# A fused two-block network on one core: two-operand operations moved from GpSimd to VectorE, and a planner's lateness for accumulating transfers

## The chip, the cores and the metric

The kernel runs on one core of a Trainium2 chip, as one program. The metric is the device time of one execution in microseconds (us). A core has TensorE (matrix products, shown as PE; its weight loads as PEld), VectorE (DVE), ScalarE (ACT), GpSimd (POOL) and SyncE (SP), each with a queue that runs in the order in which the program put it. SyncE issues most transfers, GpSimd the indirect and the accumulating ones.

## The reference

What is computed, cut to its outline (S = D = 1024, float32 throughout):

```python
def reference(...):
    x = first_block(x, w_in, conv_w, ..., w_out, ln_g, ln_b)     # 2 x hybrid_layer
    return second_block(x, c_2, ada_w_2, ..., moe_w_down_2)
...
def hybrid_layer(x, ...):
    proj = x @ w_in
    o_dn  = gated_delta_rule_chunked(l2norm(conv q), l2norm(conv k), v, g, beta)   # 4 heads
    o_gla = gla_chunked(gq, gk, gv, log_f)                                         # 4 heads, in pairs
    y = concat(head_rms_norm(o_dn) * silu(z), head_rms_norm(o_gla) * silu(z)) @ w_out
    return layer_norm(ALPHA * x + y)
...
def second_block(x, c, ...):
    for i in range(2):
        sh1, sc1, g1, sh2, sc2, g2 = split(silu(c) @ ada_w[i] + ada_b[i], 6)
        h = x * (1 + sc1) + sh1
        y = neighbourhood_mixer(h) if i == 0 else gqa_mixer(h)
        x = layer_norm_2(ALPHA * x + (1 + g1) * y)
        h = x * (1 + sc2) + sh2
        y = hierarchical_moe(h)              # top 2 of 32 experts, by groups
        x = layer_norm_2(ALPHA * x + (1 + g2) * y)
    return x
```

## The kernel before

Activations are kept as 128-row tiles of 1024 columns in 47 slots of SBUF ("slot"); narrow values are in one tile "small", PSUM is one tile "banks". A float32 product is made of three faster ones: each operand is split into a rounded high part and the rest. `split` (line 441) does that, the high part on ScalarE, the low part by a subtraction on VectorE, or on GpSimd where `pool` is set.

The stages follow each other: two mixer layers (delta rule heads in `delta_head`, gated linear attention pairs in `gla_pair`, with a projection feed at low priority between them), neighbourhood attention (`na_tile`: eight pairs of heads, eight tiles each), a first expert layer, grouped-query attention (`normed` and `normed_half` for the rotary step, `gqa_tile`), a second expert layer. Beside them `modulation` multiplies ada_w by c, 84 VectorE operations that name `c_act`. Between layers `out_proj_ln` makes the output projection by row tiles; each tile is normalised, put into DRAM by `Rows.put` and, by `Next.post` and `fill_xt` (line 585), turned and split into the next layer's input. `Rows.put` multiplies the tile on VectorE and sends it by an accumulating transfer of GpSimd's queue to a buffer `xb` or `Y`; the slot is given back when the planner believes that the transfer has ended.

Nothing of this order is written out by hand. The work is written as coroutines, and `Flow` runs them against planned clocks of the engines: `spend` asks when the operands are ready, takes a gap on the engine or its end, and sets the planned end; the coroutine that can go on first, in order of priority, is taken next. Costs are functions: `dve_cost` is 0.065 + columns / 955 us, `pool_cost` 0.05 + columns / 480 for an operation on two operands. A transfer of GpSimd costs 1.04 us of its queue and is counted as landed some us later ("late", line 76). The plan has no notion of one engine slowing another. A buffer is chosen by its planned free time. So a changed cost or engine moves instructions on all engines.

Operations of GpSimd on two operands stand in `solve` (lines 928 and 944), `norms` (1023), `delta_head` (1039, 1080, 1116), `gla_pair` (1218, 1225, 1288), `na_tile` (1925: the mask added to the position bias), `normed_half` (2116, 2117) and in `split` for the layer whose `Next` has `pool` set, which is the one after the first expert layer; and in `moe_ln` at the very end, which stay. In the trace all of them have line 72, the recording helper's, so they are told apart by tile and shape.

## Time and profile before

| what | value |
|---|---|
| median of 3 runs | 4102.42 us (4100.18 to 4103.45) |
| the profiled execution, its own time | 4100.02 us |
| its span, first to last instruction | 4098.2 us |
| TensorE busy | 3826.4 us, 93% |
| VectorE busy | 3145.8 us, 77% |
| ScalarE busy | 2207.1 us, 54% |
| GpSimd busy | 756.7 us, 18% |
| mean granted TensorE clock | 0.967 |

Busy time is the share of a whole span of unlike stages, so it is read by stretch. Where TensorE is busy nearly all the time, an operation of another engine matters only if TensorE ends up waiting for it. A wait is put down to the engine whose signal came last. An operation that is stretched by a neighbour still counts as busy.

### The profile page before, as it was taken

To read this page: it belongs to the slowest core of one execution; us is meant where nothing else is said; L and a number is where in the kernel's file an instruction comes from. 1 tells how busy PE (TensorE), PEld (TensorE's weight loads), DVE (VectorE), ACT (ScalarE), POOL (GpSimd) and SP (SyncE) were. 2 spreads that over 40 slices of the span, in tenths; PEclk is the share of its full clock that TensorE was granted. 3 is DMA by queue.
4 is the path that set the end of the run, shared out by engine and by line. 5 is a ranking of instruction groups with operands and counts; after the bars stand their busy time and mean duration, and the time that the engine had idled before them with its cause. 6 is when DMAs were issued, how large, how long until landed. Compare 5 with 4: busy or idle time off the path is not lost. (4 is left out here: it accounts for less than half of the span.)

```text
span 4098.2 us, 62930 instructions
## 1 busy us (share of the span) xinstructions
PE 3826.4 (93%) x23000; PEld 3123.1 (76%) x23000; DVE 3145.8 (77%) x5986; ACT 2207.1 (54%) x3931; POOL 756.7 (18%) x608
## 2 busy tenths in 40 slices
PE   7999998999999999999799999789999987999996
PEld 6888787788888777777677777687777875777774
DVE  7777775776775687867888899866658766888887
ACT  4333343433333455442477777567778615777773
POOL 2111100211210222321222222320000011222212
PEclk9999999999999999999899999899999997999998
DMA  4223424211123544327899999610001476999993
GB/s 154 75 85 102 146 87 101 48 38 47 50 78 111 130 139 129 114 98 231 280 366 365 368 369 379 173 23 22 22 6 65 146 200 256 359 360 368 366 363 136
DMA packets 347117, 712.56 MB, mean 174 GB/s; under 512 B 60884, under 2 KB 191630, under 8 KB 346804
## 3 DMA queue, kind: packets, MB, share of 16 engines
q1 hardware_dynamic: 320308, 645.99, 44.0%
q0 software_dynamic: 26496, 62.51, 7.4%
q8 instruction: 182, 2.98, 0.3%
q14 instruction: 131, 1.07, 0.1%
HBM read 626.94 MB, written 115.44 MB: 181 GB/s over the span
## 5 line engine op out<-in xcount | busy, mean ns | idle before, releaser
L72 PE MATMUL banks<-slot 128*128 128x512 f32 (+9 forms) x18258 | 3231.3, 343 | 81.9 <-ACT slot L72 55.6
L72 PEld LDWEIGHTS banks<-slot 128*128 128x128 f32 (+5 forms) x18258 | 2547.4, 177 | 625.7 <-issue 96.9
L72 DVE TENSOR_TENSOR slot<-slot 128x1024 fp32r<-128x1024 f32 (+13 forms) x1445 | 1360.0, 964 | 245.1 <-ACT slot L72 168.2
L72 ACT ACTIVATE slot<-slot 128x1024 fp32r<-128x1024 f32 (+5 forms) x1011 | 998.1, 1016 | 630.0 <-DVE slot L72 193.3
L72 ACT ACTIVATE slot<-banks 128x512 f32<-128x512 f32 (+8 forms) x1124 | 552.4, 513 | 673.5 <-PE banks L72 611.1
L72 PE MATMUL banks<-c,slot 128*128 128x128 f32 (+2 forms) x3484 | 510.3, 283 | 93.7 <-DVE slot L72 24.0
L72 PEld LDWEIGHTS banks<-c,slot 128*128 128x128 f32 (+1 forms) x3484 | 426.3, 158 | 195.8 <-issue 53.1
L72 DVE TENSOR_TENSOR slot<-banks,slot 128x512 fp32r<-128x512 f32 (+4 forms) x622 | 360.6, 608 | 91.7 <-ACT slot L72 48.3
L72 POOL TENSOR_TENSOR slot<-slot 128x384 f32<-128x384 f32 (+2 forms) x184 | 225.6, 1251 | 982.3 <-PE banks L72 416.8
L72 ACT ACTIVATE slot<-slot,small 128x1024 f32<-128x1024 f32 (+1 forms) x292 | 266.4, 926 | 184.5 <-DVE small L72 168.1
L72 DVE COPY slot<-banks 128x512 f32<-128x512 f32 (+6 forms) x406 | 220.0, 551 | 101.6 <-PE banks L72 81.1
L72 POOL DMA_INDIRECT Y<-slot,small x62 | 146.0, 2354 | 354.7 <-DVE slot L72 232.4
L72 ACT ACTIVATE slot<-banks,small 128x1024 f32<-128x1024 f32 x140 | 156.9, 1124 | 66.4 <-DVE small L72 65.9
L72 DVE TENSOR_REDUCE small<-banks 128x1 f32<-128x1024 f32 x128 | 154.7, 1221 | 41.7 <-PE banks L72 40.1
L72 PE MATMUL banks<-slot,small 128*128 128x512 f32 (+2 forms) x388 | 156.1, 524 | 23.3 <-ACT small L72 15.0
L72 POOL MEMSET slot<- 128x1024 f32 (+1 forms) x70 | 67.6, 968 | 578.2 <-PE banks L72 371.1
L72 POOL DMA_DIRECT2D xb<-slot x40 | 35.1, 885 | 725.2 <-DVE slot L72 581.3
L72 DVE SCALAR_TENSOR_TENSOR slot<-slot,c_act 128x1024 f32<-128x1024 f32 x84 | 119.7, 1426 | 34.5 <-DMA slot<-in_ada_w 26.2
L72 DVE SCALAR_TENSOR_TENSOR small<-small 128x1 f32<-128x1 f32 (+3 forms) x590 | 120.1, 211 | 11.7
L72 DVE TENSOR_TENSOR slot<-slot,banks 128x512 f32<-128x512 f32 (+4 forms) x110 | 72.7, 666 | 72.5 <-PE banks L72 72.4
L72 PE MATMUL banks<-small,slot 128*128 128x128 f32 (+1 forms) x576 | 105.2, 297 | 21.0 <-DVE small L72 17.6
L72 ACT ACTIVATE small<-banks 128x64 f32<-128x64 f32 (+2 forms) x289 | 78.7, 273 | 76.9 <-PE banks L72 69.6
(131 smaller groups left out, 1811.6 us busy)
## 6 DMA issues: line engine op xcount, KB each, us to landing
slot<-in_moe_w_up SPq DMA_DIRECT2D x260, 512.0 KB
slot<-in_moe_w_gate SPq DMA_DIRECT2D x260, 512.0 KB
slot<-in_moe_w_down SPq DMA_DIRECT2D x260, 512.0 KB
slot<-in_ada_w SPq DMA_DIRECT2D x96, 512.0 KB
slot<-in_w_in SPq DMA_DIRECT2D x56, 512.0 KB
xb<-slot SPq DMA_DIRECT2D x40, 512.0 KB
xb<-slot POOLq DMA_DIRECT2D x40, 512.0 KB, 5.6
slot<-xb SPq DMA_DIRECT2D x24, 512.0 KB
```

The costliest lines, as they stand in the source:

```text
L72: r = real(*a, **k)
```

## The change

Every GpSimd operation on two operands listed above is issued on VectorE instead, with the same operands; the `pool` option of `split`, `fill_xt` and `Next` is gone. In `spend`'s call a transfer that accumulates by `accum_op` (those of `Rows.put`) counts as 12 us on its way in the plan, as those with `compute_op` (the experts' indirect ones) already did; before it was 3. The operations of `moe_ln` stay on GpSimd.

```diff
@@ Engine.__getattr__
-            self._flow.spend(self._name, self._cost(op, a, k), outs, ins, (12.0 if "compute_op" in k else 3.0) if "dma" in op else 0.0)
+            self._flow.spend(self._name, self._cost(op, a, k), outs, ins, (12.0 if "compute_op" in k or "accum_op" in k else 3.0) if "dma" in op else 0.0)
@@ split
-        (F.gpsimd if pool else F.vector).tensor_sub(lo, src, hi.bitcast(F32))
+        F.vector.tensor_sub(lo, src, hi.bitcast(F32))
@@ solve
-    F.gpsimd.tensor_mul(L, D, spread(sL[:, cs], 128))
+    F.vector.tensor_mul(L, D, spread(sL[:, cs], 128))
...
-        F.gpsimd.tensor_mul(M, L, rep(K.dnm, 4))
+        F.vector.tensor_mul(M, L, rep(K.dnm, 4))
@@ norms
-    F.gpsimd.tensor_mul(sq.f, x.f, x.f)
+    F.vector.tensor_mul(sq.f, x.f, x.f)
@@ delta_head
-            F.gpsimd.tensor_mul(g2[n].rrows(), rep(K.after, NT), spread(P.g2[n][:, h], 128))
+            F.vector.tensor_mul(g2[n].rrows(), rep(K.after, NT), spread(P.g2[n][:, h], 128))
...
@@ na_tile
-            F.gpsimd.tensor_add(
+            F.vector.tensor_add(
...
@@ normed_half
-        F.gpsimd.tensor_mul(v(z, a, 0), v(x, a, 1), tb(1))
-        F.gpsimd.tensor_mul(v(z, a, 1), v(x, a, 0), tb(3))
+        F.vector.tensor_mul(v(z, a, 0), v(x, a, 1), tb(1))
+        F.vector.tensor_mul(v(z, a, 1), v(x, a, 0), tb(3))
@@ whole
-            N.pool = True
```

The programs differ in the order of all engines; TensorE's instructions are the same in number. Three places on VectorE's queue follow, before and then after. In the rows "c32" with "g" is the mask times the gates (`delta_head`), small_66 the narrow values, banks_67 PSUM, ISA the masked score step with its row minimum.

The first place is VectorE in the first mixer layer: the end of a head's normalisation (`head_out`), steps of 128x8 elements that end in the scaling of 128x512, for which TensorE's transposes wait. Before:

```order
L72 SCALAR_TENSOR_TENSOR small_66<-small_66 128x8 x2
L72 TENSOR_TENSOR small_66<-small_66 128x8
L72 SCALAR_TENSOR_TENSOR small_66<-small_66 128x8 x2
L72 TENSOR_TENSOR slot_1529<-slot_2516,slot_1529 128x1024
L72 TENSOR_TENSOR small_66<-small_66 128x8
L72 SCALAR_TENSOR_TENSOR slot_2446<-slot_2549,c_act_79,slot_2446 128x1024
L72 SCALAR_TENSOR_TENSOR small_66<-small_66 128x8
L72 TENSOR_TENSOR slot_1799<-slot_1936,slot_1799 128x1024
L72 SCALAR_TENSOR_TENSOR small_66<-small_66 128x8
L72 TENSOR_TENSOR small_66<-small_66 128x8
L72 TENSOR_TENSOR slot_1935<-slot_1935,small_66 128x512 x2
```

After:

```order
L72 SCALAR_TENSOR_TENSOR small_66<-small_66 128x8
L72 TENSOR_TENSOR slot_2557<-slot_2554,slot_2556 128x1024
L72 TENSOR_TENSOR small_66<-small_66 128x8
L72 TENSOR_TENSOR slot_1592<-slot_1938,slot_1592 128x1024
L72 SCALAR_TENSOR_TENSOR small_66<-small_66 128x8
L72 TENSOR_TENSOR slot_2598<-c32_68,g00_131 128x1024
L72 SCALAR_TENSOR_TENSOR small_66<-small_66 128x8
L72 TENSOR_TENSOR slot_2600<-c32_68,g10_132 128x1024
L72 TENSOR_TENSOR small_66<-small_66 128x8
L72 SCALAR_TENSOR_TENSOR slot_2455<-slot_2456,banks_67 128x512
L72 TENSOR_TENSOR slot_1937<-slot_1937,small_66 128x512 x2
```

Two products c32 by g, which before stood on GpSimd's queue, stand between the steps; a product that adds to the modulation has left.

The second place is VectorE where the first expert layer ends and row tiles are normalised (steps of 128x1) and split. Before:

```order
L72 SCALAR_TENSOR_TENSOR small_66<-small_66 128x1
L72 TENSOR_SCALAR small_66<-small_66 128x1
L72 TENSOR_TENSOR slot_22146<-slot_22146,banks_67 128x1024
L72 SCALAR_TENSOR_TENSOR small_66<-small_66 128x1 x2
L72 TENSOR_TENSOR slot_22491<-slot_22140,slot_16705 128x1024
L72 SCALAR_TENSOR_TENSOR small_66<-small_66 128x1 x4
L72 TENSOR_SCALAR small_66<-banks_67,cols2_11370 128x128
L72 SCALAR_TENSOR_TENSOR small_66<-small_66 128x1 x4
L72 BN_STATS small_66<-slot_22146 128x6
L72 SCALAR_TENSOR_TENSOR small_66<-small_66 128x1 x2
L72 TENSOR_SCALAR small_66<-banks_67,cols2_11370 128x128
```

After:

```order
L72 TENSOR_TENSOR slot_22144<-slot_22144,banks_67 128x1024
L72 TENSOR_SCALAR small_66<-small_66 128x1
L72 TENSOR_TENSOR slot_22544<-slot_22535,slot_22543 128x1024
L72 SCALAR_TENSOR_TENSOR small_66<-small_66 128x1
L72 TENSOR_TENSOR slot_22199<-small_66,slot_22198 128x128
L72 SCALAR_TENSOR_TENSOR small_66<-small_66 128x1
L72 TENSOR_TENSOR slot_22201<-small_66,slot_22200 128x128
L72 SCALAR_TENSOR_TENSOR small_66<-small_66 128x1
L72 TENSOR_TENSOR slot_22203<-small_66,slot_22202 128x128
L72 SCALAR_TENSOR_TENSOR small_66<-small_66 128x1
L72 TENSOR_TENSOR slot_22205<-small_66,slot_22204 128x128
L72 SCALAR_TENSOR_TENSOR small_66<-small_66 128x1
```

The 128x128 rows that write a slot from small and a slot are the low parts of the split; they stood on GpSimd's queue before and now alternate with the steps.

The third place is VectorE at the end of neighbourhood attention, behind seven low parts of the output projection's weights (the last two are shown). Before:

```order
L72 TENSOR_TENSOR slot_15211<-slot_15201,slot_15210 128x1024
L72 TENSOR_TENSOR slot_15218<-slot_15208,slot_15217 128x1024
L72 ISA slot_15239,small_66<-banks_67,slot_15239 128x384
L72 ISA small_66 128x1
L72 ISA slot_15239,small_66<-banks_67,slot_15239 128x384
L72 ISA small_66 128x1
L72 ISA slot_15260,small_66<-banks_67,slot_15260 128x384
L72 ISA small_66 128x1
L72 RECIPROCAL small_66<-small_66 128x1
L72 ISA slot_15260,small_66<-banks_67,slot_15260 128x384
L72 ISA small_66 128x1
L72 TENSOR_SCALAR slot_15239<-slot_15239,small_66 128x384
```

After:

```order
L72 TENSOR_TENSOR slot_15211<-slot_15201,slot_15210 128x1024
L72 TENSOR_TENSOR slot_15218<-slot_15208,slot_15217 128x1024
L72 TENSOR_TENSOR slot_15239<-slot_15034,slot_11372 128x384
L72 TENSOR_TENSOR slot_15239<-slot_15036,slot_11372 128x384
L72 ISA slot_15239,small_66<-banks_67,slot_15239 128x384
L72 ISA small_66 128x1
L72 ISA slot_15239,small_66<-banks_67,slot_15239 128x384
L72 ISA small_66 128x1
L72 TENSOR_TENSOR slot_15260<-slot_15034,slot_11372 128x384
L72 RECIPROCAL small_66<-small_66 128x1
L72 TENSOR_TENSOR slot_15260<-slot_15036,slot_11372 128x384
L72 TENSOR_SCALAR slot_15239<-slot_15239,small_66 128x384
```

The masked sums (128x384 from two slots) of a tile now stand ahead of its score steps on the same queue, and those of the next tile between its softmax steps.

## Rows read from the trace of the kernel before

**Rows 1.** Busy time by stretch: stretch, its us, each engine's busy us (instructions), TensorE's clock.
```profile
0.00:1390.00 1390.00, 1299.91 (x8538) 1097.70 (x8538) 995.39 (x2347) 521.48 (x1210) 202.32 (x132) 0.97 0.30 88
1390.00:1860.00 470.00, 454.05 (x2721) 359.70 (x2721) 369.26 (x884) 239.93 (x529) 144.04 (x131) 0.98 0.39 123
2300.00:2400.00 100.00, 99.09 (x443) 78.17 (x443) 90.25 (x94) 74.32 (x89) 23.47 (x16) 1.00 1.00 369
2610.00:2660.00 50.00, 31.52 (x151) 23.99 (x150) 49.42 (x159) 33.43 (x91) 28.67 (x48) 0.80 0.54 108
2660.00:3110.00 450.00, 419.45 (x3530) 355.27 (x3530) 292.12 (x553) 340.72 (x796) 44.38 (x65) 0.98 0.09 27
```

**Rows 2.** TensorE's waits, 0 to 1390: waited for, us in total, times, longest.
```profile
PE banks L72 <- DVE slot L72: 21.7, 16, 4.2
...
PE banks L72 <- DVE small L72: 17.6, 14, 3.3
```

**Rows 3.** Timeline at 289: start, us, engine, operation, tiles, shape [idle before <-releaser].
```profile
289.46 0.16 DVE L72 SCALAR_TENSOR_TENSOR small<-small 128x8 f32<-128x8 f32 x1
289.54 1.22 DVE L72 TENSOR_TENSOR slot<-slot 128x1024 f32<-128x1024 f32 x1
289.68 2.87 POOL L72 TENSOR_TENSOR slot<-c,g 128x1024 fp32r<-128x1024 f32 x1 [8.12 <-DVE small L72]
...
290.67 1.89 DVE L72 SCALAR_TENSOR_TENSOR small<-small 128x8 f32<-128x8 f32 x1
...
293.63 0.63 PE L72 MATMUL banks<-c,slot 128*128 128x128 f32 x4 [4.18 <-DVE slot L72]
```

**Rows 4.** VectorE's groups by shape, 0 to 1390: count, busy us, mean ns, idle before.
```profile
L72 DVE TENSOR_TENSOR slot<-slot 128x512 f32<-128x512 f32 x104 | 91.2, 911 | 3.2 <-PE banks L72 1.6 <-ACT slot L72 1.5
```

**Rows 5.** VectorE's groups by shape, whole span.
```profile
L72 DVE TENSOR_TENSOR slot<-slot 128x1024 f32<-128x1024 f32 x96 | 116.2, 1219 | 18.6 <-ACT slot L72 15.2 <-DMA slot<-in_na_w_o 3.2
...
L72 DVE CUSTOM_DVE_ANT_0 slot<-banks,slot 128x384 f32<-128x384 f32 x128 | 67.6, 547 | 4.9 <-PE banks L72 3.2 <-POOL slot L72 1.6
...
L72 DVE SCALAR_TENSOR_TENSOR slot<-slot 128x512 f32<-128x512 f32 x48 | 33.0, 688 | 15.8 <-ACT slot L72 15.4
...
L72 DVE TENSOR_TENSOR slot<-small,slot 128x128 fp32r<-128x128 f32 x128 | 30.7, 291 | 16.0 <-ACT slot L72 15.7
...
L72 DVE COPY slot<-banks 128x256 f32<-128x256 f32 x32 | 13.4, 420 | 15.2 <-ACT slot L72 15.1
```

**Rows 6.** GpSimd's groups by shape, whole span.
```profile
L72 POOL TENSOR_TENSOR slot<-slot 128x384 f32<-128x384 f32 x112 | 126.5, 1158 | 296.0 <-PE banks L72 151.8 <-DMA slot<-in_rpb_lay 96.3 <-DVE slot L72 35.6
```

**Rows 7.** VectorE's waits, 0 to 1390.
```profile
DVE small L72 <- POOL slot L72: 18.7, 14, 3.0
```

**Rows 8.** Timeline at the end of neighbourhood attention, from 1837.
```profile
1837.66 8.03 DVE L72 TENSOR_TENSOR slot<-slot 128x1024 fp32r<-128x1024 f32 x7
...
1839.33 11.61 POOL L72 TENSOR_TENSOR slot<-slot 128x384 f32<-128x384 f32 x6 [36.53 <-PE banks L72]
...
1846.49 0.56 DVE L72 CUSTOM_DVE_ANT_0 slot<-banks,slot 128x384 f32<-128x384 f32 x1 [0.80 <-POOL slot L72]
...
1847.12 0.90 PE L72 MATMUL banks<-c,slot 128*128 128x128 f32 x3 [5.80 <-DVE small L72]
```

**Rows 9.** Timeline of GpSimd at the last splits after the first expert layer.
```profile
2663.13 7.30 POOL L72 TENSOR_TENSOR slot<-small,slot 128x128 fp32r<-128x128 f32 x16
```

**Rows 10.** Timeline at one rotary step of grouped-query attention, from 2803.
```profile
2803.41 4.83 DVE L72 TENSOR_TENSOR slot<-slot 128x256 f32<-128x256 f32 x6 [6.00 <-PE banks L72]
...
2808.89 0.88 PE L72 MATMUL banks<-slot 128*64 128x128 f32 x12 [1.79 <-DVE slot L72]
```

**Rows 11.** SyncE's own queue: waited for, us in total, times, longest.
```profile
SPq L185 <- DMA xb<-slot: 110.6, 12, 21.9
```

**Rows 12.** Timeline at the two changes of layer, at 710 and 1391.
```profile
710.45 1.06 ACT L72 ACTIVATE slot<-slot 128x1024 fp32r<-128x1024 f32 x1 [7.64 <-DMA slot<-in_w_in]
...
718.44 1.22 PE L72 MATMUL banks<-slot 128*128 128x512 f32 x2 [11.69 <-ACT slot L72]
...
1390.97 1.74 PE L72 MATMUL banks<-slot 128*128 128x512 f32 x3 [9.91 <-ACT slot L72]
```

More of the change, by code (lines that the diff above doesn't have):

```diff
@@ L438, in rsqrt, with split @@
     K.small.give(b)
-def split(K, hi, lo, src, scale=None, pool=False):
+def split(K, hi, lo, src, scale=None):
     F = K.F
@@ L582, in turn, with fill_xt @@
     K.banks.give(*ps)
-def fill_xt(K, X, x, t, cols=None, pool=False):
+def fill_xt(K, X, x, t, cols=None):
     F = K.F
@@ L607, in fill_xt @@
             s = slice(t * 128, (t + 1) * 128)
-            split(K, X.hi[k].r[:, s], X.lo[k].r[:, s], src.f[:, j * 128:(j + 1) * 128], pool=pool)
+            split(K, X.hi[k].r[:, s], X.lo[k].r[:, s], src.f[:, j * 128:(j + 1) * 128])
         K.banks.give(p)
@@ L1079, in delta_head @@
         K.banks.give(p)
-        F.gpsimd.tensor_mul(atv, atv, rep(K.upto, 4))
+        F.vector.tensor_mul(atv, atv, rep(K.upto, 4))
         yield
@@ L1115, in delta_head @@
     with F.aside():
-        F.gpsimd.tensor_mul(kr.rows(), kr.rows(), spread(P.eK[:, h], 128))
+        F.vector.tensor_mul(kr.rows(), kr.rows(), spread(P.eK[:, h], 128))
     o = yield from A.take(user)
@@ L1217, in gla_pair @@
     x = yield from A.take(user)
-    F.gpsimd.tensor_mul(x.f, k.f, q.f)
+    F.vector.tensor_mul(x.f, k.f, q.f)
     yield
@@ L1224, in gla_pair @@
         with F.aside():
-            F.gpsimd.tensor_mul(at[i].rows(), rep(K.ident, NT), spread(dg.f[:, i * NT:i * NT + NT], 128))
+            F.vector.tensor_mul(at[i].rows(), rep(K.ident, NT), spread(dg.f[:, i * NT:i * NT + NT], 128))
     K.small.give(dg)
@@ L1287, in gla_pair @@
     F.scalar.activation(x.f[:, 0:512], x.f[:, 0:512], AF.Exp)
-    F.gpsimd.tensor_mul(t, pairs(k)[:, :, 0], pairs(q)[:, :, 1])
+    F.vector.tensor_mul(t, pairs(k)[:, :, 0], pairs(q)[:, :, 1])
     V.tensor_mul(t, t, x.f[:, 0:512])
@@ L1660, in __init__ @@
     def __init__(self, K, name, order, g, b, mod=None):
-        self.K, self.X, self.pool = K, XT(K), False
+        self.K, self.X = K, XT(K)
         self.X.user = K.A.user(order, 0)
@@ L1670, in post @@
             self.K.A.leave(self.X.user)
-        yield from fill_xt(self.K, self.X, x.f, t, self.cols, self.pool)
+        yield from fill_xt(self.K, self.X, x.f, t, self.cols)
 def first_block(K, x_dram, x_bufs):
```

## The prediction

> **What bounds the kernel now.** I first cut the span into stretches [rows 1]. In the two mixer layers of the first block (0 to 1390) TensorE is busy 1299.91 of 1390 us, in neighbourhood attention (1390 to 1860) 454.05 of 470, in grouped-query attention (2660 to 3110) 419.45 of 450, and in the middle of the first expert layer (2300 to 2400) 99.09 of 100. TensorE is the bound nearly everywhere, so only what shortens or lengthens its waits counts. One short stretch is different: from 2610 to 2660, where the first expert layer ends and the next layer's input is split, VectorE is busy 49.42 of 50 us and TensorE 31.52.
>
> Then I asked who ends TensorE's waits. In the mixer layers VectorE ends 16 + 14 of them, 39.3 us in all [rows 2]. GpSimd ends none directly. It acts through VectorE: an operation of 128x8 elements that takes 0.16 us took 1.89 us while a GpSimd multiply of 2.87 us ran beside it, and 4.18 us of TensorE waiting ended at its chain [rows 3]. The same shows in the means: VectorE's 128x512 products of two slots take 911 ns in the mixer layers [rows 4], the same size with nothing beside it 688 ns [rows 5]. So a two-operand operation on GpSimd is not free for VectorE. How much of its price comes back is the question.
>
> **Part 1: 336 operations change engine.** They are 52 of 128x1024 and 52 of 128x512 in the mixer layers, 128 of 128x384 in neighbourhood attention, 64 of 128x128 in the split after the first expert layer, 40 of 128x256 in the rotary step of grouped-query attention. On GpSimd one of 384 columns takes 1158 ns [rows 6]. On VectorE I take 1219, 688, 547, 291 and 420 ns from the rows of the same sizes, the last from a copy, since the 128x256 products never run alone [rows 5]. That is 52 x 1.219 + 52 x 0.688 + 128 x 0.547 + 64 x 0.291 + 40 x 0.420 = 63.4 + 35.8 + 70.0 + 18.6 + 16.8 = 205 us more on VectorE. It is paid only where a TensorE wait stands behind it. By stretch:
>
> *Mixer layers.* VectorE gets 99 us more in 1390, where it is busy 995.39 [rows 1]. Back comes at least 104 x (0.911 - 0.688) = 23 us of stretched products [rows 4, 5]. VectorE also stood still for GpSimd 14 times, 18.7 us [rows 7], above all for the squares of the norms; that goes. But the order of the changed program puts the multiply that stood beside the chain at 290 into the chain itself, twice: 2 x 1.22 = 2.4 us between steps of 0.16 us, where the stretch had cost 1.89 - 0.16 = 1.73. So stretch and added work nearly cancel, and what is left is the 18.7 us of standing still. I let a quarter of it reach TensorE, since VectorE idles for 395 us here and most of that is slack: -5 us. Bounds: half of the 39.3 us goes (-20), or an added operation lands before each of the 30 waits, 30 x 1.22 = 37, less the quarter that the relief gives back (23 of 99): +28.
>
> *Neighbourhood attention.* 70 us more in 470; VectorE goes from 369.26 to about 439, 93%. In the expert layer it is busy 90.25% with TensorE at 99.09% [rows 1], so such a share need not show. It shows where no projection work is left to fill TensorE, at the end. There seven 128x1024 products held VectorE for 8.03 us, GpSimd's six masks took 11.61 us beside them, and TensorE waited 5.80 us [rows 8]. In the changed order the first two masks stand right behind the same seven products and four more between the steps of the softmax. The long wait stays, and the masks add 6 x 0.547 = 3.3 us to VectorE where it waited at most 0.80 us for GpSimd. I take +2. Bounds: 0, and +16, if TensorE's share falls from 96.6% here to the 93.2% that it has in grouped-query attention (3.4% of 470).
>
> *Split after the first expert layer.* VectorE is full and gets 64 x 0.291 = 18.6 us. Against that, GpSimd's last ones came late, sixteen of them from 2663 on [rows 9], in a stretch where VectorE has room again [rows 1]. 48 x 0.291 = 14 stay; ends overlap by 0.09 (289.54 + 1.22 against a next start at 290.67 [rows 3]), so 9.7 in the queue. The order puts them between the short steps of the normalisation, and such steps can be stretched beside GpSimd, by 1.73 us for the one at 290 [rows 3]; a few of them given back would pay for most of it. I take +3; bounds -5 and +13 (the 14 without relief). By the Trainium skill (Perfetto Trace Analysis, "Optimizing Scalar/DVE Operations") offloading from a saturated VectorE to GpSimd may make sense, though the two share a read port; that speaks against moving these 64, and with +13 in place of +3 the sum below would be +3.
>
> *Grouped-query attention.* Ten rotary steps, each four VectorE products beside four on GpSimd. The six VectorE operations took 4.83 us, and a copy that TensorE waited 1.79 us for came behind them [rows 10]. On VectorE alone it is 8 x 0.420 + 2 x 0.688 = 4.7 us by durations; ends overlap in the queue, so about 3.9. That is 0.1 to 0.9 us for each of ten, and the wait of GpSimd's last product goes. -5; bounds -9 and +2.
>
> **Part 2: accumulating transfers planned 12 us instead of 3.** This is a number in the planner; it moves only when a buffer counts as free. SyncE's queue stood 12 times for such a transfer, 110.6 us, at most 21.9 [rows 11]. Counted over the built programs, loads of SyncE into a buffer whose last reader is an accumulating transfer fall from 61 to 31. What does it buy? The two long TensorE waits between layers, 11.69 us at 718 and 9.91 at 1391, end on ScalarE, which had waited for weights (7.64 us for the first) [rows 12]. But the load in question at 700 waited for TensorE and for GpSimd's memset, not for an accumulating transfer. At 1391 the load behind the 21.9 us was not that of the weights used first; these still stand behind six mask loads, whose buffers TensorE frees late. So -2 for both; bounds -12 (the 9.91 and some) and +4 (three weight loads of grouped-query attention now go into buffers of such transfers, which before did none). The expert layers keep their order: 0.
>
> **The sum.** -5 + 2 + 3 - 5 - 2 = -7 us. The profiled execution took 4100.0 us (span 4098.2 and 1.8 around it), 2.4 under the median of the runs shown, 4102.4. So 4100.0 - 7 = 4093 for it, 4095 for a median like theirs. What this kernel's measurement can tell from no change is about 0.2%, 8.2 us.
>
> **The rivals.**
> 1. *VectorE's queue becomes the chain (slower).* In the mixer layers the added operations land between the small steps that TensorE waits for, as the order shows at one place: +28 instead of -5, so +26 with the rest, 4128. For it: in-order queue, VectorE ends 30 waits. Against: 395 us of idle VectorE time in the stretch, and the standing still for GpSimd that goes. It decides itself where more than one in two of the 30 waits has an added operation just ahead.
> 2. *The relief is worth more (faster).* Half of the 39.3 us goes in the mixer layers and the full 9 in grouped-query attention: -20 + 2 + 3 - 9 - 2 = -26, 4076. For it: the stretched step of 290 stood in the chain of a 4.18 us wait [rows 3]. Against: the same order.
> 3. *Nothing reaches TensorE (it does not do what it says).* Both the 205 us and the relief lie in VectorE's idle time: 0, 4102. For it: GpSimd ends no TensorE wait.
> 4. *The full stretch at 2610 pays everything:* +13 there, +3 in all, 4105.
>
> **How the numbers follow.** Forecast 0.42, with its own range -17 to +3, as the rows of the four small terms are uncertain by some 10 us together; about half of it lies beyond -8.2. Rival 1: 0.22. Rival 2: 0.18. Rival 3: 0.11. Rival 4: 0.07. Faster by over 0.2%: 0.20 + 0.18 = 0.38. Within: 0.22 + 0.11 + 0.06 = 0.39. Slower: 0.22 + 0.01 = 0.23. The range runs from 4072, a little beyond rival 2, to 4124, which leaves out the upper half of rival 1.
>
> **What the next profile would show.** Right: VectorE's mean for 128x512 products back near 690 ns, no VectorE wait for GpSimd, VectorE busy about 110 to 160 us more, TensorE's waits for VectorE in the mixer layers within 5 us of 39, SyncE's waits for accumulating transfers well below 110 us with the two waits between layers still there. Wrong: TensorE's share in 1390 to 1860 below 95%, or waits for VectorE above 50 us in the mixer layers (rival 1), or below 25 (rival 2), or TensorE idle above 30 us where now 18.5 of 50 are (rival 4). If the time moves by more than 15 us, the new order itself, and not the price of the operations, has moved TensorE's waits, and I would have read the wrong rows.

## The result, and the profile after

The changed kernel takes 4057.7 us (median; 4051.5 to 4066.6) beside 4102.9 (4100.2 to 4104.4) of the kernel before. The ratio is 0.990, with the interval 0.988 to 0.991: faster by about 1%. I had forecast 4095 with a range down to 4072, so the direction was right and the size was not.

TensorE's busy time is the same as before (3826.4 us), so the gain is idle time of TensorE. The engines of the whole span, from the page of the changed kernel:

```profile
PE 3826.8 (94%) x23000; PEld 3123.5 (77%) x23000; DVE 3218.6 (79%) x6322; ACT 2211.5 (55%) x3929; POOL 363.1 (9%) x272
```

Where the time went is read by stretch. The stretches are cut at events that both kernels have: the last row statistics of each layer and the last score step of neighbourhood attention, all on VectorE. In order: the two mixer layers, neighbourhood attention, its output projection, the first expert layer with the split, grouped-query attention with its projection, the second expert layer, the end. The columns are the stretch, its length in us, the busy time of TensorE, its weight loads, VectorE, ScalarE and GpSimd (with instructions), TensorE's granted clock, the share of the DMA engines and GB/s. The kernel before:

```profile
0.00:1391.50 1391.50, 1300.44 (x8539) 1098.20 (x8540) 996.89 (x2355) 522.98 (x1211) 202.32 (x132) 0.97 0.30 88
1391.50:1861.30 469.80, 454.81 (x2733) 360.23 (x2732) 369.06 (x880) 239.31 (x529) 144.04 (x131) 0.98 0.39 123
1861.30:1977.90 116.60, 115.06 (x651) 95.29 (x649) 85.29 (x230) 23.44 (x32) 14.05 (x16) 1.00 0.84 245
1977.90:2650.20 672.30, 626.87 (x2781) 493.68 (x2781) 589.67 (x755) 468.09 (x588) 170.77 (x134) 0.96 0.93 337
2650.20:3370.40 720.20, 678.75 (x5464) 567.22 (x5462) 490.83 (x988) 492.32 (x1028) 64.41 (x89) 0.98 0.23 68
3370.40:4052.60 682.20, 632.46 (x2796) 499.32 (x2796) 573.77 (x669) 451.30 (x538) 142.33 (x98) 0.96 0.90 328
```

The changed kernel:

```profile
0.00:1348.90 1348.90, 1289.32 (x8546) 1087.81 (x8546) 1018.77 (x2476) 525.61 (x1221) 20.98 (x30) 0.98 0.31 90
1348.90:1839.10 490.20, 466.87 (x2729) 368.35 (x2730) 414.27 (x988) 236.85 (x517) 0.87 (x1) 0.96 0.38 120
1839.10:1952.90 113.80, 113.50 (x647) 94.79 (x645) 84.59 (x228) 23.23 (x31) 13.94 (x16) 1.00 0.81 237
1952.90:2621.20 668.30, 621.70 (x2760) 490.19 (x2759) 591.09 (x791) 465.56 (x590) 148.98 (x100) 0.96 0.94 341
2621.20:3343.00 721.80, 688.39 (x5483) 573.52 (x5483) 497.15 (x1060) 495.52 (x1025) 16.54 (x19) 0.98 0.23 68
3343.00:4007.10 664.10, 625.98 (x2787) 497.87 (x2787) 570.65 (x669) 455.25 (x538) 143.05 (x98) 0.96 0.92 336
```

Three stretches matter. The mixer layers are 42.6 us shorter: 31.5 of it is idle time of TensorE (91.1 to 59.6), and 11.1 is busy time, as the same products ran at a mean clock of 0.98 in place of 0.97. (8.1 of these 11.1 us lie in the second mixer layer; the other 3.0 are less than the first layer varies from run to run, see below.) Neighbourhood attention is 20.4 us *longer*. The second expert layer is 18.1 us shorter. The others are within 4 us.

In the mixer layers VectorE has 99 us more work by the prediction's count, yet its busy time rises by only 21.9 us. Products of 128x512 elements, 911 ns before [rows 4], are back at 684. The groups of VectorE by shape (count, busy us, mean ns, idle before) have in 0 to 1390:

```profile
L72 DVE TENSOR_TENSOR slot<-slot 128x512 f32<-128x512 f32 x108 | 70.8, 684 | 2.1 <-ACT slot L72 1.9
```

And TensorE's waits that VectorE ends there fall from 39.3 us [rows 2] to 13.2 (waited for, us in total, times, longest; 6.0 of it is one wait between the layers):

```profile
PE banks L72 <- DVE slot L72: 8.5, 8, 6.0
...
PE banks L72 <- DVE small L72: 4.7, 2, 2.8
```

The second expert layer holds a gain that I had put at zero: 11.6 of its 18.1 us are idle time of TensorE, 6.5 busy time. TensorE's waits for ScalarE's narrow values there, before and then after:

```profile
PE banks L72 <- ACT small L72: 14.4, 29, 1.4
```

```profile
PE banks L72 <- ACT small L72: 2.4, 2, 2.2
```

Its timeline shows why (start, us, engine, operation, tiles, shape, count; in brackets the idle time before and what ended it). Before, eight transposes stand in a row; TensorE then starts a product whose operand ScalarE is still copying out, waits, and makes four more transposes behind it:

```profile
3471.49 1.11 PE L72 MATMUL banks<-c,slot 128*128 128x128 f32 x8
3473.07 1.13 PE L72 MATMUL banks<-slot,small 128*128 128x512 f32 x2 [0.47 <-ACT small L72]
3474.03 0.60 PE L72 MATMUL banks<-c,slot 128*128 128x128 f32 x4
```

After, all twelve stand in a row, and the copy is done when the product starts:

```profile
3465.14 1.66 PE L72 MATMUL banks<-c,slot 128*128 128x128 f32 x12
3466.64 1.88 PE L72 MATMUL banks<-slot,small 128*128 128x512 f32 x4
```

### The profile page after: what moved, and what is told of

Read it like the earlier page. It is cut to its first block, busy times and chain, and to the rows that moved or that the text cites. A ratio compares the mean times of both kernels' runs of the same rounds, so it can differ in the third digit from the quotient of the medians.

```text
span 4054.6 us, 62542 instructions
## 1 busy us (share of the span) xinstructions
PE 3826.8 (94%) x23000; PEld 3123.5 (77%) x23000; DVE 3218.6 (79%) x6322; ACT 2211.5 (55%) x3929; POOL 363.1 (9%) x272
## 5 line engine op out<-in xcount | busy, mean ns | idle before, releaser
L72 PE MATMUL banks<-slot 128*128 128x512 f32 (+7 forms) x18258 | 3240.2, 343 | 64.5 <-ACT slot L72 44.8
L72 PEld LDWEIGHTS banks<-slot 128*128 128x128 f32 (+4 forms) x18258 | 2548.3, 176 | 610.1 <-ACT slot L72 90.7
L72 DVE TENSOR_TENSOR slot<-slot 128x1024 fp32r<-128x1024 f32 (+13 forms) x1621 | 1398.7, 891 | 169.0 <-ACT slot L72 107.8
L72 ACT ACTIVATE slot<-banks 128x512 f32<-128x512 f32 (+9 forms) x1124 | 550.2, 511 | 711.5 <-PE banks L72 657.3
L72 PEld LDWEIGHTS banks<-c,slot 128*128 128x128 f32 (+1 forms) x3484 | 424.5, 157 | 195.6 <-ACT slot L72 42.6
L72 DVE COPY slot<-banks 128x512 f32<-128x512 f32 (+7 forms) x406 | 220.5, 551 | 88.1 <-PE banks L72 78.8
L72 DVE TENSOR_REDUCE small<-banks 128x1 f32<-128x1024 f32 x128 | 155.0, 1220 | 45.4 <-PE banks L72 44.3
L72 DVE SCALAR_TENSOR_TENSOR slot<-slot,c_act 128x1024 f32<-128x1024 f32 x84 | 107.4, 1278 | 20.9 <-DMA slot<-in_ada_w 20.1
L72 DVE SCALAR_TENSOR_TENSOR slot<-banks,cw,slot 128x511 f32<-128x511 f32 (+1 forms) x144 | 106.8, 744 | 6.9 <-ACT slot L72 5.1
```

The costliest lines, as they stand in the source:

```text
L72: r = real(*a, **k)
```

## The experiments

Every comparison below is of stretches cut at the same events. One profiled execution stands for each kernel, and the first mixer layer, with the same instructions in the same order, came out at 684, 689 and 696 us in e12, e9 and e3 (nearly all of it busy time of TensorE, 645.8 to 657.2), so a difference under some 10 us in one stretch is read only where several kernels agree. The stretches in us (both mixer layers; attention; its projection; first expert layer and split; grouped-query attention; second expert layer), then the median time and the ratio to the kernel before on the same chip, whose medians there were 4096.0 to 4102.9:

| kernel | mixer | attn | proj | exp 1 | gqa | exp 2 | median | ratio (interval) |
|---|---|---|---|---|---|---|---|---|
| before | 1391.5 | 469.8 | 116.6 | 672.3 | 720.2 | 682.2 | 4102.9 | 1 |
| changed | 1348.9 | 490.2 | 113.8 | 668.3 | 721.8 | 664.1 | 4057.7 | 0.990 (0.988 to 0.991) |
| e1 number only | 1376.0 | 473.4 | 133.0 | 669.0 | 727.1 | 665.5 | 4095.9 | 1.000 (0.998 to 1.001) |
| e2 engines only | 1352.3 | 484.7 | 127.3 | 669.9 | 730.6 | 685.4 | 4091.0 | 0.999 (0.997 to 1.000) |
| e3 old plan, VectorE | 1346.5 | 476.1 | 116.9 | 669.6 | 723.5 | 682.8 | 4061.7 | 0.990 (0.987 to 0.993) |
| e4 new plan, GpSimd | 1394.3 | 478.1 | 116.1 | 665.1 | 718.7 | 666.0 | 4092.1 | 0.999 (0.997 to 1.000) |
| e5 attention back | 1349.7 | 470.4 | 141.4 | 668.7 | 718.1 | 666.8 | 4062.9 | 0.990 (0.988 to 0.993) |
| e6 echoes on GpSimd | 1401.1 | 487.6 | 115.7 | 666.6 | 720.1 | 664.3 | 4109.9 | 1.002 (1.001 to 1.003) |
| e7 chain products | 1372.5 | 469.8 | 116.5 | 672.6 | 720.9 | 683.9 | 4084.6 | 0.996 (0.995 to 0.997) |
| e8 products ahead | 1360.4 | 468.7 | 116.7 | 670.1 | 720.7 | 681.1 | 4070.1 | 0.993 (0.991 to 0.996) |
| e9 mixer and split only | 1339.8 | 469.5 | 117.5 | 666.9 | 730.2 | 665.6 | 4039.7 | 0.986 (0.984 to 0.988) |
| e10 attention on GpSimd, new plan | 1350.5 | 480.1 | 115.2 | 670.0 | 722.8 | 666.7 | 4049.8 | 0.988 (0.986 to 0.990) |
| e11 only attention moved | 1400.3 | 472.9 | 116.7 | 670.9 | 719.7 | 684.7 | 4106.2 | 1.003 (1.002 to 1.004) |
| e12 as e9, number later | 1334.2 | 469.1 | 116.6 | 671.5 | 719.6 | 665.9 | 4032.9 | 0.986 (0.983 to 0.988) |

### Each part alone

e1 is the kernel before with one line changed:

```diff
-            self._flow.spend(self._name, self._cost(op, a, k), outs, ins, (12.0 if "compute_op" in k else 3.0) if "dma" in op else 0.0)
+            self._flow.spend(self._name, self._cost(op, a, k), outs, ins, (12.0 if "compute_op" in k or "accum_op" in k else 3.0) if "dma" in op else 0.0)
```

> The kernel before with the one number of the planner changed: accumulating transfers count as 12 us on their way. No operation changes engine. In the built program TensorE's order in the second expert layer changes as in the changed kernel (twelve transposes in a row where the kernel before has eight, then four). Theory A (this number earns only the second expert layer; the engine moves earn the mixer layers): second expert layer about 15 us shorter (596 to 581 between the landmarks), both mixer layers within 5 us of before, time 4083 to 4090. Theory B (the number also frees the waits between the mixer layers): second mixer layer 10 to 25 us shorter too, time 4062 to 4078. If the number does nothing: 4102.

e2 is the changed kernel with that line as before.

> All 336 operations on VectorE, the planner's number for accumulating transfers back at 3. Theory A: both mixer layers 35 to 45 us shorter together than before, neighbourhood attention 15 to 20 us longer, second expert layer unchanged at 596 us (eight and four transposes), time 4068 to 4078. Theory B (the mixer layers gain from the number): mixer layers at most 15 us shorter, attention 15 to 20 longer, time 4095 to 4110.

The expectations count the second expert layer between inner landmarks, 596 us before; the table has the whole of it. There the gain is the number's, as theory A has it (682.2 to 665.5 in e1, 685.4 in e2), and the moves alone shorten the mixer layers (1391.5 to 1352.3).

The other half of theory A failed. In e1 the mixer layers are 15.5 us shorter too, with no operation moved: the second of them went from 673.0 to 653.2, as theory B had it. The two long waits between the layers are gone there. TensorE's waits for ScalarE's slots in both mixer layers, before and then in e1:

```profile
PE banks L72 <- ACT slot L72: 30.5, 8, 11.7
```

```profile
PE banks L72 <- ACT slot L72: 9.5, 7, 2.8
```

But neither part brought a whole-time gain of note: 0.1% at most, where A had 0.4% and 0.7%, and B for the number 0.6% or more. Each gave its gain back elsewhere: attention's projection came out at 133.0 and 127.3 where the kernel before has 116.6, and grouped-query attention at 727.1 and 730.6 in place of 720.2. These two stretches hold the same operations in both kernels but for the rotary products. What differs is the plan, and with it the order of SyncE's loads (e5 below shows one such case; e2's was not followed up). Together the two stretches are 23.3 and 21.1 us longer than before in e1 and e2, and 1.2 shorter in the changed kernel. So the two parts do not add up: apart they bring 0.2% in all, joined 1.0%. What is missing apart lies in these two stretches, which the planner happened to lay out worse with either part alone.

### Price or order

The changed program differs in two things: who executes the 336 operations, and the plan made from it. e3 and e4 separate them. In e3 the planner counts GpSimd's clock and cost as before, and only the instruction goes to VectorE; in e4 it is the other way round. (The framework sorts a little after the planner, so the orders agree but for shifts of a few places.) The diff is that of e3; e4 is the changed kernel with `Engine(self, "DVE", nc.gpsimd, dve_cost)` in its place.

```diff
         self.gpsimd = Engine(self, "POOL", nc.gpsimd, pool_cost)
+        self.moved = Engine(self, "POOL", nc.vector, pool_cost)
...
-    F.gpsimd.tensor_mul(sq.f, x.f, x.f)
+    F.moved.tensor_mul(sq.f, x.f, x.f)
...
```

> The plan of the kernel before, buffers and all (GpSimd's clock and cost for the moved operations), but their instructions are issued on VectorE; only small shifts of order remain (1745 of 19470 TensorE instructions moved, nearly all by 20 places or fewer). Theory price (what VectorE no longer loses beside GpSimd shortens its chains): mixer layers 30 to 45 us shorter, second expert layer unchanged, time 4060 to 4080. Theory order (the new plan is what pays): mixer layers within 10 us of before or longer, since 99 us of work stand in VectorE's queue where no plan allowed for them, time 4098 to 4125.

> The plan of the changed kernel (VectorE's clock and cost, 12 us for accumulating transfers), but the 336 operations are issued on GpSimd. Theory price: mixer layers back to within 10 us of before (718 and 673), second expert layer 581, attention back near 470, time 4085 to 4095. Theory order: mixer layers 30 to 45 us shorter as in the changed kernel, attention 470 to 490, time 4045 to 4062.

In the mixer layers the answer is clean. Executed on GpSimd: 1391.5 with the old plan, 1394.3 with the new. On VectorE: 1346.5 and 1348.9. It is the price of the operations, 45 us, and the order is worth no more than a run varies (2 to 3). Theory order falls. This holds for this pair of plans: e1's plan, which keeps GpSimd's products and frees the waits between the layers, has 1376.0. In the second expert layer it is the plan alone: 682.2 and 682.8 with the old, 664.1 and 666.0 with the new, whoever executes.

The place that the prediction argued from shows what I missed. In e3 the chain of small steps of [rows 3] does have two products of c and g between its steps, as the order showed for the changed kernel. A part of its timeline on VectorE:

```profile
270.03 1.23 DVE L72 TENSOR_TENSOR slot<-c,g 128x1024 fp32r<-128x1024 f32 x1
271.17 0.18 DVE L72 SCALAR_TENSOR_TENSOR small<-small 128x8 f32<-128x8 f32 x1
...
272.45 1.24 DVE L72 TENSOR_TENSOR slot<-c,g 128x1024 fp32r<-128x1024 f32 x1
273.59 0.18 DVE L72 TENSOR_TENSOR small<-small 128x8 f32<-128x8 f32 x1
...
281.18 1.28 DVE L72 TENSOR_TENSOR slot<-slot,small 128x512 f32<-128x512 f32 x2
```

No step of this place is stretched (0.18 where one took 1.89), and the scaling that TensorE waits for starts at 281.18. Before it started at 292.80:

```profile
292.80 1.29 DVE L72 TENSOR_TENSOR slot<-slot,small 128x512 f32<-128x512 f32 x2
```

That is 11.6 us earlier with more work in the queue, and TensorE's wait of 4.18 us is gone. The chain itself did become longer: from its first small step to the scaling it took 15.6 us (from 265.56), before 10.3 (from 282.55). But it began 17.0 us earlier. By then 21 operations of VectorE had been stretched in the kernel before, by 23.6 us in all (how they are counted is said below), and TensorE had waited 9.4 us for VectorE, in e3 1.8. So what the relief buys is summed over the queue, and what the products cost in the chain is paid once.

### Is it interference, or the way through GpSimd?

Two mechanisms could make the price: GpSimd's products slow VectorE's, or results simply came late from a slower engine (VectorE stood 18.7 us for them [rows 7]). e7 and e8 cut the 104 products of the mixer layers in two, by about equal GpSimd time (GpSimd's busy time in the two layers is 202 us before, 115 and 111 here). Both have the old plan and the `moved` of e3. The diff is one line of e7, which has `sq`, `L`, `atv`, `x` and `t` so; e8 has `M`, `g2`, `kr` and `at`.

```diff
-    F.gpsimd.tensor_mul(sq.f, x.f, x.f)
+    F.moved.tensor_mul(sq.f, x.f, x.f)
...
```

> The plan of the kernel before; of the mixer layers' 104 products only the 56 that the next step waits for (squares of the norms, decay and score masks, the products of the gated pairs) are issued on VectorE, the 48 that are made ahead stay on GpSimd, and so does all else. Theory latency: nearly the whole 45 us of the mixer layers (old plan, all moved: 1346.5 against 1391.5) comes with these, mixer layers 1345 to 1356, time 4058 to 4070. Theory interference: about half of GpSimd's time remains, so about half of the gain, mixer layers 1362 to 1378, time 4072 to 4086.

> The counterpart: only the 48 products that are made ahead (gates, block masks, scaled keys, diagonals) are issued on VectorE, the 56 of the chain stay on GpSimd. Theory latency: 0 to 8 us of the mixer layers' gain, mixer layers 1383 to 1395, time 4090 to 4104. Theory interference: half of it or more, since these run beside foreign VectorE work, mixer layers 1362 to 1375, time 4070 to 4084.

The 48 products that nobody waits for at once bring 31.1 us, the 56 of the chain 19.0 (median times 4070.1 and 4084.6); together 50, which is the 45 of e3 within what a run varies. VectorE still stands 14.0 us for GpSimd's slots in e8, where the gain is larger, and not at all in e7. So a product of GpSimd costs mainly because it runs, and little because it is waited for. e6 is the counter-test: the changed kernel, with every moved product made once more on GpSimd into a scratch.

```diff
+def echo(K, n, a, b):
+    for c in range(0, n, 3):
+        m = min(3, n - c)
+        o = K.scratch[:, 0:128 * m].rearrange("p (c j) -> p c j", j=128)
+        K.nc.gpsimd.tensor_mul(o, a[:, c:c + m], b[:, c:c + m])
...
     F.vector.tensor_mul(sq.f, x.f, x.f)
+    echo(K, 8, x.rows(), x.rows())
...
```

> The changed kernel, and beside every moved product of the mixer layers GpSimd makes the same product once more (in pieces of 384 columns) into a scratch that nobody reads. TensorE's and SyncE's orders are those of the changed kernel. Theory interference (VectorE is slowed while GpSimd runs a two-operand product): most of the gain goes, mixer layers 1375 to 1395 in place of 1349, time 4082 to 4105. Theory latency (what counted was that results came from GpSimd, slow and a hop away): nothing waits for the echoes but a buffer now and then, mixer layers 1349 to 1358, time 4054 to 4066.

All of the gain went, and more: the mixer layers took 1401.1 us. TensorE's waits in them:

```profile
PE banks L72 <- DVE small L72: 23.9, 13, 4.3
...
PE banks L72 <- DVE slot L72: 21.5, 17, 6.0
```

45.4 us end on VectorE again, as the 39.3 did before, though VectorE waited for an echo's tile only 3 times, 2.7 us. They are 32.2 of the 39.0 us by which TensorE's idle time is longer than in the changed kernel. Its own work is stretched: with the same instructions as in the changed kernel its busy time is 1089.00 us in place of 1018.77.

```profile
0.00:1401.10 1401.10, 1302.55 (x8546) 1096.04 (x8546) 1089.00 (x2476) 523.82 (x1221) 281.11 (x290) 0.97 0.30 87
```

The 128x512 products of two slots are at 834 ns and those of a slot and a narrow tile at 825 (685 in the changed kernel), while an operation with one operand in PSUM stays at 744 (745):

```profile
L72 DVE TENSOR_TENSOR slot<-slot 128x512 f32<-128x512 f32 x108 | 87.1, 834 | 1.9 <-ACT slot L72 1.8
...
L72 DVE TENSOR_TENSOR slot<-slot,small 128x512 f32<-128x512 f32 x48 | 38.0, 825 | 1.3 <-ACT slot L72 1.0
...
L72 DVE SCALAR_TENSOR_TENSOR slot<-banks,cw,slot 128x511 f32<-128x511 f32 x48 | 35.6, 744 | 3.3 <-ACT slot L72 2.7
```

The dose is larger than before's (the echoes are in short pieces, GpSimd is busy for 281 us where it was for 202), so e6 shows the mechanism and not its exact size.

The records of the traces show the same one operation at a time. Call an operation of VectorE stretched when it takes over 0.15 us longer than the median of the same operation, tiles and shape in e3, where GpSimd makes no products. Counted so in the mixer layers:

| kernel | stretched operations | by us in all | TensorE's waits for VectorE, us | mixer layers, us |
|---|---|---|---|---|
| e6 | 146 | 72.0 | 45.4 | 1401.1 |
| before | 56 | 65.8 | 40.7 | 1391.5 |
| e7 | 35 | 42.2 | 32.1 | 1372.5 |
| e8 | 29 | 29.4 | 26.8 | 1360.4 |
| changed | 1 | 0.3 | 13.2 | 1348.9 |

(The 40.7 are the 39.3 of [rows 2] and one wait of 1.4 for another tile.) The 911 ns of the 128x512 products before is a mixture: 25 of the 104 overlap a GpSimd product in time and take 1629 ns on average, the other 79 take 683. And 65 operations that read PSUM began inside a GpSimd product; none of them took even 0.01 us longer than in e3. Interference holds; latency alone does not.

### Attention: where the change loses

e5 puts the masked sums and the rotary products back on GpSimd, in plan and queue; e10 keeps the changed kernel's plan and only issues them on GpSimd; e11 is the kernel before, old plan, with nothing but the masked sums issued on VectorE. The diff is that of e5 (`na_tile` and `normed_half`); e10 has the `moved` of e4 there, e11 that of e3.

```diff
-            F.vector.tensor_add(
+            F.gpsimd.tensor_add(
...
-        F.vector.tensor_mul(v(z, a, 0), v(x, a, 1), tb(1))
+        F.gpsimd.tensor_mul(v(z, a, 0), v(x, a, 1), tb(1))
```

> The changed kernel with two of its moves undone: the masked sums of neighbourhood attention and the rotary products stand on GpSimd again, in plan and queue. The mixer layers, the split and the 12 us stay as changed. If these two moves cost what the two-by-two of the earlier runs says (neighbourhood attention 6 to 12 us, rotary products 3), attention falls from 490 to 470 to 480, the grouped-query stretch from 722 to about 718, the mixer layers stay at 1345 to 1355 and the second expert layer at 666: time 4030 to 4046. If the loss in attention came from the new plan and not from the price, attention stays at 485 to 490 and the time at 4052 to 4060.

> The changed kernel's plan (GpSimd not used in it for these operations), but the masked sums and the rotary products are issued on GpSimd. If attention's loss is VectorE's price for them: attention about 478 as in the run of the new plan on GpSimd, its projection 116 (not the 141 that the re-planned version had), grouped-query stretch 719, time 4038 to 4050. If the loss is the new plan's: attention stays near 490, time 4053 to 4062.

> The plan of the kernel before, and only the 128 masked sums of neighbourhood attention issued on VectorE. Theory queue (they stand ahead of the score steps on VectorE and nothing comes back): attention 475 to 482 in place of 470, all other stretches within 5 us of before but for what a run varies, time 4102 to 4112 where the kernel before has 4098 to 4102. Theory interference here too (GpSimd's products stretched VectorE's in attention as they did in the mixer layers): attention 455 to 467, time 4085 to 4097.

In attention the moved sums cost time in every pair. With the old plan: 469.8 to 472.9 (e11) and 476.1 (e3). With the new: 480.1 (e10) and 478.1 (e4) to 490.2. That is 3 to 6 us and 10 to 12. The new plan itself costs some 8 to 10 (470 to 478 and 480); e5, whose plan counts the sums on GpSimd again, has 470.4. e11 is slower than the kernel before as a whole, by 0.3%; of its 12.6 us more between first and last event only 3.1 lie in attention, and 8.8 in the mixer layers, whose work and order are those of before, so the whole time overstates it, and where the rest comes from stays open. Interference is little help in attention: by the count above GpSimd's 128 sums, 144.5 us of its time, stretch VectorE there by 9.3 us, against 65.8 us for 183.8 in the mixer layers. The score steps, which have one operand in PSUM, take 547 ns before and 544 in e11.

How the loss looks in the changed kernel is seen near 1580. TensorE has three longer waits, for slots that ScalarE and VectorE write:

```profile
1581.04 0.98 PE L72 MATMUL banks<-slot 128*128 128x384 f32 x4 [1.29 <-ACT slot L72]
...
1584.64 0.90 PE L72 MATMUL banks<-c,slot 128*128 128x128 f32 x3 [1.37 <-DVE slot L72]
1586.12 2.93 PE L72 MATMUL banks<-slot 128*128 128x512 f32 x6 [0.58 <-ACT slot L72]
```

and the granted clock of the 20 us in which that happens is 0.83, after 1.00 in those before (columns as above):

```profile
1560.00:1580.00 20.00, 19.75 (x134) 14.90 (x132) 17.38 (x60) 11.01 (x30) 0.00 (x0) 1.00 0.26 80
1580.00:1600.00 20.00, 16.79 (x103) 12.68 (x104) 16.95 (x38) 7.18 (x17) 0.00 (x0) 0.83 0.48 148
```

So a part of those 20 us ran at the lower level of 1.2 GHz. In the whole stretch 12.1 us of the 20.4 are longer busy time of the same products, 8.3 are waits.

e5 won attention back (470.4) and lost it in the next stretch, 141.4 in place of 113.8. SyncE stood there for a buffer that the last masked sums on GpSimd were reading, with the loads of the attention's output behind it (SyncE's own queue, 1780 to 1965):

```profile
SPq L185 <- POOL slot L72: 29.7, 1, 29.7
```

TensorE then waited 8.40 us at 1850 for the first of them. e1 has the same wait there (26.2 us) and 133.0 us. As I read it, this is neither price nor interference but a load in the wrong place of a queue in order. SyncE's waits for the accumulating transfers to Y stand in the same queue (55.6 us from 1780 to 1965, changed kernel 28.2 in its place), and no run parts the two.

### A better version

e9 takes what the runs had shown to pay: the old plan, VectorE for the mixer layers' products and the split (with the `moved` of e3), GpSimd for the rest, the 12 us from the second block layer on. e12 is e9, but sets them only behind the routing of the second expert layer, in `block_2_layer`; of its diff this part is shown.

```diff
     M = yield from moe_front(K, l, user, R, Bump(kept))
+    if l == 1:
+        F.late = 12.0
```

> The plan of the kernel before. Only the mixer layers' products and the split after the first expert layer are issued on VectorE; neighbourhood attention and the rotary products stay on GpSimd. The 12 us hold only from the second block layer on, where the built program shows twelve transposes in a row. If the stages add up as the runs so far give them: mixer layers 1346, attention 470, its projection 117, first expert layer with its split 670, grouped-query stretch 720, second expert layer 666, end 47, sum 4036, time 4032 to 4046, below the changed kernel. If the order around the second layer's transfers shifts as it did for the projection in the run with the number alone: 4050 to 4065.

> The kernel of the ninth run, with the 12 us set only after the routing of the second expert layer has begun, so that the plan up to there is that of the kernel before. The built program still has the twelve transposes in a row. If the 12 us cost what the grouped-query stretch showed (730 against 720 with the same operations): that stretch 719 to 724, second expert layer 664 to 668, time 4026 to 4038. If the 730 came from the run and not from the number: stretch 725 to 732, time 4036 to 4044.

Both fell where the sum of stretches put them, e9 with some luck: its mixer layers came out 6 us below what was put in, grouped-query attention 10 above. e12 takes 4032.9 us beside 4096.0 of the kernel before on the same chip, 0.986 (0.983 to 0.988), below the changed kernel's 0.990 (0.988 to 0.991); the intervals just part (0.9881 and 0.9883). In grouped-query attention 719.6 against 730.2 of e9 agrees with the number's cost there, though the two whole times (4032.9 and 4039.7, on different chips, ratios 0.986 both) do not tell e9 and e12 apart. The run also shows that the accumulating transfers behind the second routing are enough to turn the order of the second expert layer. Why the planner then takes twelve transposes in a row I did not follow up.

## Why the prediction was wrong, by its own steps

**Mixer layers: right sign, far too small.** Forecast -5 (bounds -20 to +28), measured -42.6, and -45.0 with the order held. The step that failed is "stretch and added work nearly cancel". I took from the order that two products enter the chain and set 2.4 us against one stretched step of 1.73. The chain's timeline in e3 shows both products there, the chain itself 5.4 us longer, and its end 11.6 us earlier. One place had been weighed for itself, where the queue ahead of it carried the stretch of everything before.

The relief was mis-sized as well: "at least 23 us" came from the 128x512 products alone. VectorE's busy time gives the whole. The added products come to 99.2 us by their durations, and to some 90 in a queue where ends overlap by 0.09. So 996.9 + 90 = 1087 us were to be expected in the mixer layers. e3 has 529.8 + 478.4 = 1008.2 in its two:

```profile
0.00:696.40 696.40, 657.24 (x4308) 552.21 (x4308) 529.84 (x1269) 273.68 (x634) 10.27 (x15) 0.96 0.37 110
696.40:1346.50 650.10, 632.03 (x4231) 534.48 (x4231) 478.36 (x1193) 251.37 (x577) 9.44 (x13) 0.99 0.24 69
```

So nearly 80 us came back of the 90 added; the count of stretched operations alone has 65.8. I had the group of one shape, and took a lower bound as the value.

The clock was missing too: 11.1 of the 42.6 us are the same products at a higher mean clock. The 8.1 of them in the second layer are the surer part: TensorE is busy there for 631 to 632 us in all seven kernels that have these products on VectorE without echoes, and for 640.0 before. No term of the sum had a price for what a wait does to the stretch behind it.

**Rival 2** was the right mechanism, and its size (-20) was half of what came; its mark, waits for VectorE below 25 us, was met with 13.2. **Rival 1** is refuted: the order does put the added operations between the small steps, and at the place of [rows 3] no wait follows. **Rival 3** and **rival 4** did not come either; for rival 4, TensorE is idle for 19.8 us in the 50 that had 18.5.

**Neighbourhood attention:** forecast +2 (0 to +16), measured +20.4. The kind was right and the size wrong, above the upper bound. The price (3 to 12) lies inside it; the plan's part (8 to 10) I had no term for. The place was wrong too: at the end of the stretch the long wait is 4.90 us where it was 5.80, and the added waits lie spread over it, as near 1580.

**Split:** forecast +3, measured -4.0 for its stretch; issued on VectorE against GpSimd it is -2.7 with the old plan and +3.2 with the new, so about nothing. The Trainium skill (Perfetto Trace Analysis, "Optimizing Scalar/DVE Operations") allows offloading from a saturated VectorE, and warns that between these two engines it might not help; here GpSimd's help on a VectorE busy for 49.42 of 50 us [rows 1] was worth no more than that.

**Grouped-query attention:** forecast -5, measured +1.6. Between runs that differ in where the products are issued it is +3.3 (e3 against before), +3.1 (changed against e4) and -1.0 (changed against e10), so the price is not told from nothing. The waits did go as forecast, with the old plan: TensorE's waits for VectorE's slots fall from 14.0 to 8.4 us in e3. But its busy time there is 6.3 us longer (678.75 to 685.00); some of that is 13 more of its products inside the cut, and the cause of the rest stays open.

**Part 2:** forecast -2, and "the expert layers keep their order: 0". This failed outright. The order of TensorE in the built program has twelve transposes where eight and four had been, in the second expert layer alone; I had looked only at the three places shown for VectorE. It is worth -18.1 here, and -15 to -18 in every kernel that has the number there. Between the layers, where I looked for its gain, -2 was too small for the number alone: e1's mixer layers are 15.5 us shorter and both long waits are gone, beyond even the bound of -12. In the changed kernel, whose plan is another, the waits moved rather than went: 11.69 us at the first change [rows 12] became 7.46 and 6.00, and the 9.91 at the second became 3.27. SyncE's waits for accumulating transfers fell from 110.6 [rows 11] to 70.9 us:

```profile
SPq L185 <- DMA xb<-slot: 70.9, 14, 9.3
```

**The marks.** Right: 684 ns for the 128x512 products (the 688 that I set it against is another operation in the same layers, 8 of whose 48 do overlap a GpSimd product, so "with nothing beside it" was not exact), no VectorE wait for GpSimd's slots in the mixer layers, SyncE's waits well below 110 us. Wrong: VectorE busy only 73 us more, not 110 to 160, since more stretch came back than I gave it; and TensorE's waits for VectorE in the mixer layers at 13.2, not within 5 of 39. One mark was blind: TensorE's share in attention stayed above its 95% (466.87 of 490.20) though the stretch lost 20 us, because its busy time grew as well. And as I wrote there, a move of more than 15 us meant that I had read the wrong rows; only the reason given, the new order, holds for the second expert layer and not for the mixer layers.

## What to carry to other kernels

In this kernel a two-operand operation given to GpSimd is paid for on VectorE by the work from SBUF, mostly on two operands, that stands in VectorE's queue at that time, and the cheap-looking ones made ahead cost as much as those in the chain. To price it, sum the stretch over the queue (all shapes, busy time expected against seen), not at one chain; and where little of VectorE's work is stretched, as in the attention here with its score steps from PSUM, try leaving the work on GpSimd. Where a planner lays the queues, compare the built order in every stage before a stage is put at zero, and test each edit once with the old plan kept, since price and plan can have opposite signs and two edits need not add up.

## What was not expected of the hardware

The stretch is all or nothing. In [rows 3] the small step starts at 290.67 and ends at 292.56; GpSimd's product beside it starts at 289.68 and ends at 292.55. The step did not run slowly: it ended when GpSimd was done. The 128x1024 product that had started first, at 289.54, took its 1.22 us as if alone, and there it was GpSimd that stood: its product took 2.87 us where nine of the sixteen of its kind take 1.89 to 1.90, so it ran from about 290.65 on, when VectorE's was ending. This is no single case. Of the 56 stretched operations before, 54 end as long after the end of a GpSimd product as they take by themselves, less 0.13 to 0.20 us; in e6 it is 145 of 146.

The Trainium skill (SBUF — State Buffer, "Who interferes with whom" and "SBUF: two separate sides") says just that: a VectorE instruction with two inputs in SBUF and a GpSimd instruction that reads SBUF block each other, and whoever starts first holds the way for the whole instruction; this trace agrees, and so does the 744 ns of the operation with one input in PSUM in e6. Nine of the 56 have a single tensor as input, a copy and eight TENSOR_SCALAR; in the trace they are stretched like the others.

By that rule, the price of GpSimd's work is up to its own duration each time. What came of it depends on what VectorE has in its queue: 65.8 us of stretch for 183.8 us of GpSimd's products in the mixer layers before, 72.0 for 260.1 us of echoes in e6, 9.3 for 144.5 in attention.

Waits were dearer than their length. In the changed kernel's attention 8.3 us of added waits went with 12.1 us of longer busy time at a mean clock of 0.96 in place of 0.98.
